# Fifteen loads of 1 to 15 short rows between the transfers of one DMA queue

## The chip, the cores and the metric

The kernel runs on one core of a Trainium2 chip. The metric is the device time of one execution in microseconds; the median of three runs is used.

## The reference

For each of 8 x 12 heads, Q, K and V are 512 x 64 in float32. The columns of Q and K are divided by their norms over the 512 rows, a 64 x 64 matrix is formed from them, a softmax runs over its last axis, and V is multiplied by the result:

```python
Q_norm = Q / (np.linalg.norm(Q, axis=-2, keepdims=True) + 1e-10)
K_norm = K / (np.linalg.norm(K, axis=-2, keepdims=True) + 1e-10)
attn = np.einsum('bhnd,bhne->bhde', Q_norm, K_norm)
attn = np.exp(attn - np.max(attn, axis=-1, keepdims=True))
attn = attn / (np.sum(attn, axis=-1, keepdims=True) + 1e-10)
return np.einsum('bhnd,bhde->bhne', V, attn)
```

Q, K and V are 12.58 MB each and so is the output: 50.3 MB pass between HBM and the core's SBUF, whatever the order of the work.

## The kernel before

The 96 heads are taken four at a time (24 units u), two units to a stage s (12 stages) and two stages to a pair w (6 pairs). A stage loads Q and K (`load_qk`, L172, one or two transfers for each), casts them to bfloat16 on VectorE (L212), forms the Gram matrices on TensorE (L232), takes norms and scores from them (L239 to L290), and multiplies by V, which `load_v` (L189) brings and which is cast (L168, L170) and transposed (L301) for it. ScalarE brings the products from PSUM (L166, L320) and `store` (L198) writes them out, 512 KB at a time.

All transfers but the first two loads of K are issued by SyncE, in one queue; those two go through ScalarE's queue. An object `Order` (L22) plans the order on every engine with costs written by hand, and the loop at L458 emits the pieces in that order. Four loads (`ahead`) are emitted before it, at L330. The loads from `HELD` on are kept back until the piece `UNTIL` has been emitted, and are then emitted in a row (L466).

The transfers are numbered here as the loop emits them: A1 to A4 are the four loads ahead of it, T1 to T67 the others, all from SyncE. T1 is the first load of V (1 MB), T2 to T5 are the four quarters of stage 1's Q and K (512 KB each), T6 is V (1 MB), T7 to T10 are the quarters of stage 2 (512 KB each), T11 to T22 are loads of 1 MB, T23 and T24 are the first two stores. A load of Q or K is 128 rows (a quarter) or 256 rows of 4 KB, a load of V 128 rows of 8 KB, a store 256 rows of 2 KB. One store near the end (T60 to T63, L202 to L204) is cut into 92, 4 and 32 rows and the other 128.

Completion is told by semaphores. The framework gives the transfers eight of them in turn, so that each transfer waits, at its issue on SyncE, until the transfer eight places ahead of it has landed, besides what its buffer needs. For the built program that reads, around the place of the change (lane numbers are the eight semaphores; the rows are the program's order on SyncE with their waits):

```
T5   L187 DMACopy qk<-in_K_dram 128x1024 [waits lane 0, DVE]
T6   L194 DMACopy v<-in_V_dram 128x2048 [waits lane 1]
T7   L187 DMACopy qk<-in_Q_dram 128x1024 [waits lane 2]
T8   L187 DMACopy qk<-in_K_dram 128x1024 [waits lane 3]
T9   L187 DMACopy qk<-in_Q_dram 128x1024 [waits lane 4]
T10  L187 DMACopy qk<-in_K_dram 128x1024 [waits lane 5]
T11  L185 DMACopy qk<-in_Q_dram 128x2x1024 [waits lane 6, DVE]
```

A transfer's rows are dealt out to as many as 16 DMA engines, each of which works through its share in order and then counts the semaphore up by one; the transfer has landed when the last engine has done so.

Of the kernel before, what the change touches and what calls it, by code (L numbers as in the profile page):

```python
# [8 lines left out]
F32 = mybir.dt.float32  # L9
# [4 lines left out]
D = 64  # L14
# [88 lines left out]
def kernel(  # L103
# [7 lines left out]
    nc = tc.nc  # L111
# [218 lines left out]
    for r in range(2):  # L330
# [7 lines left out]
        name=nc.get_next_instruction_name(), engine=mybir.EngineType.Activation, ins=[], outs=[], act_func_set_id=LN_EXP))  # L338
# [40 lines left out]
    def loaded(x, s, r):  # L379
        return ("l" + "qk"[x], s, r if len(parts(s)) == 2 else None)  # L380
# [33 lines left out]
    for w in range(W):  # L414
        both = 2 * w >= BOTH
        for r in range(2):
            halves = (None,)
            n = 2 * w + r - NB["v"]
# [22 lines left out]
    for s in range(S):  # L441
        for x in range(4):
            i, k = divmod(x, 2)
            n = 4 * s + x - 2
# [3 lines left out]
            n = 2 * s + i - NB["so"]  # L448
# [6 lines left out]

    ahead = [loaded(x, 0, r) for r in range(2) for x in range(2)]
    held, passed = [], False
    for (emit, eng), (_, _, key, _) in zip(plan.run(), plan.order):  # L458
        if eng == "DMA" and not passed and (held or key == HELD):
            held.append(emit)  # L460
            continue
        if key not in ahead:
            emit(eng)
        if key == UNTIL:
            passed = True
            for load in held:  # L466
                load("DMA")


# [28 lines left out]
```

## Time and profile before

| what | value |
|---|---|
| three runs, median (lowest to highest) | 129.33 us (129.22 to 129.61) |
| span of the profiled execution | 127.4 us |
| busy: VectorE, TensorE, ScalarE, GpSimd | 92.9, 77.0, 72.3, 37.0 us |
| moved | 50.66 MB, mean 398 GB/s |

The page gives no other time of the profiled execution than its span; the difference to the median of the runs, 1.9 us, lies around the span.

The trace also records each DMA packet and each step of a semaphore, which no view prints. Packets of the kernel's own queues have these durations (median):

| packet | count | ns |
|---|---|---|
| 4 bytes (semaphore step) | 1112 | 9 |
| 2,048 bytes (store row) | 6144 | 84 |
| 4,096 bytes (Q or K row) | 6144 | 159 |
| 8,192 bytes (V row) | 1536 | 309 |
| 16,384 bytes (a block of instructions, queue q8) | 17 | 935 |

And some transfers, in us from the start of the span: when SyncE began the issue, when the first of the 16 engines counted the semaphore up, and when the last did:

| transfer | issue begins | first engine done | last engine done |
|---|---|---|---|
| T3 | 2.85 | 12.62 | 13.05 |
| T4 | 3.33 | 13.87 | 15.45 |
| T5 | 6.70 | 15.13 | 16.69 |
| T6 | 7.08 | 17.58 | 19.13 |
| T7 | 8.46 | 18.83 | 20.35 |
| T8 | 8.83 | 20.06 | 21.57 |
| T9 | 10.61 | 21.32 | 23.16 |
| T10 | 11.82 | 22.58 | 24.23 |
| T11 | 13.12 | 25.05 | 26.68 |
| T13 | 16.70 | 30.02 | 31.70 |
| T17 | 23.22 | 39.89 | 41.48 |
| T18 | 25.66 | 42.38 | 44.02 |
| T21 | 32.38 | 49.86 | 51.40 |
| T22 | 34.21 | 52.34 | 53.88 |
| T28 | 51.05 | 64.79 | 66.58 |
| T29 | 51.77 | 67.28 | 70.22 |
| T30 | 53.90 | 69.78 | 72.67 |
| T57 | 106.62 | 113.83 | 116.85 |
| T58 | 107.89 | 115.12 | 119.65 |
| T59 | 109.22 | 116.39 | 120.69 |
| T67 (the last) | 120.75 | 123.55 | 126.53 |

For T67 the 16 engines ended at 123.6 (three), 124.3 to 125.5 (twelve) and 126.5 (one).

### The profile page before, as it was taken

To read this page: it belongs to the slowest core of one execution; us is meant where nothing else is said; L and a number is where in the kernel's file an instruction comes from. 1 tells how busy PE (TensorE), PEld (TensorE's weight loads), DVE (VectorE), ACT (ScalarE), POOL (GpSimd) and SP (SyncE) were. 2 spreads that over 40 slices of the span, in tenths; PEclk is the share of its full clock that TensorE was granted. 3 is DMA by queue.
4 is the path that set the end of the run, shared out by engine and by line. 5 is a ranking of instruction groups with operands and counts; after the bars stand their busy time and mean duration, and the time that the engine had idled before them with its cause. 6 is when DMAs were issued, how large, how long until landed. Compare 5 with 4: busy or idle time off the path is not lost.

```text
span 127.4 us, 4949 instructions
## 1 busy us (share of the span) xinstructions
PE 77.0 (60%) x2160; PEld 62.7 (49%) x2160; DVE 92.9 (73%) x142; ACT 72.3 (57%) x220; POOL 37.0 (29%) x39
## 2 busy tenths in 40 slices
PE   0065393994837679859475986777597729753000
PEld 0054372783636568647354674666386517541000
DVE  3344749949899899999974989998999499950000
ACT  4000441559877077886691897583848919996000
POOL 4006307300916903033077011303733160300000
PEclk9999999999985555999996799869959995999755
DMA  4999999999999999999999999999999999999991
GB/s 113 413 438 408 428 411 418 417 433 408 435 418 414 411 417 424 402 415 427 423 414 414 415 428 417 415 424 425 401 420 419 401 402 410 395 408 408 375 377 60
DMA packets 14958, 50.66 MB, mean 398 GB/s; under 512 B 1112, under 2 KB 1112, under 8 KB 13400
## 3 DMA queue, kind: packets, MB, share of 16 engines
q1 hardware_dynamic: 14648, 49.29, 95.9%
q10 hardware_dynamic: 288, 1.05, 2.1%
q8 instruction: 17, 0.28, 0.8%
q14 instruction: 5, 0.04, 0.1%
HBM read 37.75 MB, written 12.58 MB: 395 GB/s over the span
## 4 chain that ended last, share of the span: by engine, by line
DVE 36%; PE 21%; DMA 19%; issue 8%; ACT 5%; SPq 1%; DVEq 0%; ACTq 0%
DVE qkb L212 15%; DMA qk<-in_K_dram 14%; PE gram L232 12%; DVE scr L239 7%; DMA qk<-in_Q_dram 5%; DVE vt L168 4%; PE vps L301 4%; DVE ab L290 4%; PE po L318 3%; ACT so L166 3%; DVE n L251 2%; ACT ex L281 2%; DVE vb L168 2%; PE lg L275 1%; SPq L185 1%
## 5 line engine op out<-in xcount | busy, mean ns | idle before, releaser
L232 PE MATMUL gram<-qkb 32*128 32x128 bf16 x1536 | 36.7, 259 | 24.8 <-issue 8.5
L232 PEld LDWEIGHTS <-qkb 32*128 32x128 bf16 x1536 | 30.8, 116 | 29.7 <-issue 11.1
L212 DVE CAST qkb<-qk 128x1024 bf16<-128x1024 f32 x48 | 37.7, 810 | 9.6 <-DMA qk<-in_Q_dram 8.0
L170 POOL TENSOR_SCALAR vb<-v 128x1024 bf16<-128x1024 f32 x18 | 21.7, 1215 | 43.9 <-DMA v<-in_V_dram 39.0
L166 ACT COPY vt<-vps 128x1024 bf16<-128x1024 bf16 (+1 forms) x18 | 17.8, 986 | 18.8 <-PE vps L301 18.7
L166 ACT COPY so<-po 128x512 f32<-128x512 f32 x45 | 24.9, 593 | 6.1 <-PE po L318 5.8
L318 PE MATMUL po<-ab,vt 128*64 128x128 bf16 x384 | 19.1, 237 | 6.2 <-issue 2.6
L262 POOL TENSOR_TENSOR kqs<-kq,r 64x512 f32<-64x512 f32 x12 | 14.0, 1169 | 29.1 <-ACT r L258 16.2
L301 PE MATMUL vps<-identb,vb 128*128 128x128 bf16 x192 | 18.5, 253 | 4.8 <-POOL vb L170 3.5
L239 DVE SCALAR_TENSOR_TENSOR scr<-gram,eye 64x512 f32<-64x512 f32 x24 | 16.5, 687 | 4.9 <-PE gram L232 4.7
L318 PEld LDWEIGHTS <-vt 128*64 128x64 bf16 x384 | 13.4, 117 | 10.4 <-issue 5.7
L301 PEld LDWEIGHTS <-vb 128*128 128x128 bf16 x192 | 14.0, 113 | 7.9 <-POOL vb L170 4.2
L281 ACT ACTIVATE ex<-lg,rq 128x64 f32<-128x64 f32 x48 | 14.5, 322 | 2.7 <-PE lg L275 2.6
L166 ACT COPY kq<-gram 64x512 f32<-64x512 f32 x12 | 7.0, 582 | 13.2 <-DVE scr L239 12.9
L290 DVE TENSOR_TENSOR ab<-ex,rinv 64x256 bf16<-64x256 f32 x24 | 12.8, 534 | 0.6
L281 ACT ACTIVATION_READ_ACCUMULATOR ex<-lg,rq 128x1 f32 x48 | 10.2, 213 | 0.0
L168 DVE CAST vb<-v 128x1024 bf16<-128x1024 f32 x6 | 7.4, 1241 | 1.8 <-DMA v<-in_V_dram 1.7
L275 PE MATMUL lg<-eye,kqs 64*128 64x64 f32 x48 | 6.4, 259 | 3.2 <-issue 1.6
L251 DVE TENSOR_REDUCE n<-scr 128x8 f32<-128x512 f32 x12 | 8.1, 679 | 0.1
L168 DVE COPY vt<-vps 128x1024 bf16<-128x1024 bf16 (+1 forms) x8 | 8.0, 1022 | 0.2
L275 PEld LDWEIGHTS lg<-eye,kqs 64*128 64x128 f32 x48 | 4.5, 156 | 5.0 <-issue 2.5
L287 DVE RECIPROCAL rinv<-esum 128x4 f32<-128x4 f32 x12 | 2.0, 170 | 2.5 <-ACT ex L281 2.4
(17 smaller groups left out, 16.0 us busy)
## 6 DMA issues: line engine op xcount, KB each, us to landing
v<-in_V_dram SPq DMA_DIRECT2D x12, 1024.0 KB, 17.4
out_dram<-so SPq DMA_DIRECT2D x23, 512.0 KB, 11.2
qk<-in_Q_dram SPq DMA_DIRECT2D x8, 1024.0 KB, 16.8
qk<-in_K_dram SPq DMA_DIRECT2D x8, 1024.0 KB, 18.8
qk<-in_Q_dram SPq DMA_DIRECT2D x8, 512.0 KB, 11.9
qk<-in_K_dram SPq DMA_DIRECT2D x6, 512.0 KB, 12.6
qk<-in_K_dram ACTq DMA_DIRECT2D x2, 512.0 KB, 7.3
out_dram<-so SPq DMA_DIRECT2D x1, 256.0 KB, 7.2
```

The costliest lines, as they stand in the source:

```text
L166: nc.scalar.copy(o, i)
L168: nc.vector.tensor_copy(o, i)
L170: nc.gpsimd.tensor_scalar(out=o, in0=i, scalar1=1.0, scalar2=0.0, op0=ALU.mult, op1=ALU.add)
L212: nc.vector.tensor_copy(qkb[u][:, :, x * D:(x + 1) * D], qk32[s][:, x, r])
L232: nc.tensor.matmul(gram[s][:, h, r, 0], x, x, start=(t == 0), stop=(t == (T if u < WIDE else J) - 1))
L239: nc.vector.scalar_tensor_tensor(out=scr[s][half], in0=gram[s][half, :, :, 0, half].rearrange("p h r d -> p (h r) d"), scalar=1e-20, in1=e ...
L262: (nc.vector if eng == "DVE" else nc.gpsimd).tensor_tensor(out=kqs[s][HI], in0=kq[s][HI], in1=r8[s][HI, :, None].to_broadcast([D, 2 * HU, ...
L275: nc.tensor.transpose(l[:, h, :], kqs[s][HI, 2 * h:2 * h + 2].rearrange("p r d -> p (r d)"), eye2[HI])
L281: nc.scalar.activation(e[:, h, :], lg[s][:, h, :], AF.Exp, scale=rq[s][:, h:h + 1], accum_out=z[:, h:h + 1])
L290: nc.vector.tensor_tensor(out=a[half, :, half], in0=e[half], in1=ri[half, :, None].to_broadcast([D, HU, D]), op=ALU.mult,)
L301: nc.tensor.transpose(ps[:, c, n, :], vb[w][:, J * c + j].rearrange("p r d -> p (r d)"), identb)
L318: nc.tensor.matmul(po[s, x][e * D:(e + 1) * D, j].rearrange("p r d -> p (r d)"), v, ab[s][:, h, :])
```

## The change

Behind each of the seventh to the 21st transfer that the loop emits (T7 to T21) one small load is issued on SyncE: the n-th takes the first 16 floats (64 bytes) of the first n rows of K into the first n partitions of a tile of its own, which nothing reads. These loads take their turn among the eight semaphores like the others. They make 120 rows, 7,680 bytes, and the tiles take 15 x 64 bytes of each partition of SBUF.

```diff
     held, passed = [], False
+    marks = ctx.enter_context(tc.tile_pool(name="marks", bufs=1))
+    Km = K.rearrange("b h n d -> (b h n) d")
+    seen = [0]
+
+    def mark():
+        seen[0] += 1
+        n = seen[0] - 6
+        if 0 < n < 16:
+            m = marks.tile([128, D // 4], F32, name=f"mark{n}")
+            nc.sync.dma_start(out=m[0:n], in_=Km[0:n, 0:D // 4])
+
+    def emit_dma(emit):
+        emit("DMA")
+        mark()
+
     for (emit, eng), (_, _, key, _) in zip(plan.run(), plan.order):
...
         if key not in ahead:
-            emit(eng)
+            emit_dma(emit) if eng == "DMA" else emit(eng)
         if key == UNTIL:
             passed = True
             for load in held:
-                load("DMA")
+                emit_dma(load)
```

In the built program the order on the other engines is the same as before, and on SyncE the fifteen loads M1 to M15 stand where the diff says. Around the first of them, with the semaphore each waits for:

```
T7   L187 DMACopy qk<-in_Q_dram 128x1024 [waits lane 2]
M1   L467 DMACopy mark<-in_K_dram 1x16 [waits lane 3]
T8   L187 DMACopy qk<-in_K_dram 128x1024 [waits lane 4]
M2   L467 DMACopy mark<-in_K_dram 2x16 [waits lane 5]
T9   L187 DMACopy qk<-in_Q_dram 128x1024 [waits lane 6]
M3   L467 DMACopy mark<-in_K_dram 3x16 [waits lane 7]
T10  L187 DMACopy qk<-in_K_dram 128x1024 [waits lane 0]
M4   L467 DMACopy mark<-in_K_dram 4x16 [waits lane 1]
T11  L185 DMACopy qk<-in_Q_dram 128x2x1024 [waits lane 2, DVE]
```

## Prediction

> **What bounds the kernel now.** First the page: its span, the slices, and the queues.
>
> ```profile
> span 127.4 us, 4949 instructions
> ...
> DMA  4999999999999999999999999999999999999991
> ...
> q1 hardware_dynamic: 14648, 49.29, 95.9%
> ...
> DVE 36%; PE 21%; DMA 19%; issue 8%; ACT 5%; SPq 1%; DVEq 0%; ACTq 0%
> ```
>
> The DMA engines are busy in all slices but the first and the last, and the kernel's own queue q1 alone takes 95.9% of the 16 engines' span. The chain of waits in the fourth of these lines gives VectorE 36%, but it ends with a copy at 116.6 us, before the last stores drain, so it isn't what ends the kernel. The windows by stage settle it (the columns are the stretch, its length, busy us of PE, PEld, DVE, ACT and POOL with counts, granted clock, DMA share, GB/s):
>
> ```profile
> 12.00:24.00 12.00, 6.81 (x188) 5.64 (x192) 9.29 (x16) 4.67 (x18) 4.09 (x4) 1.00 1.02 418
> 24.00:36.00 12.00, 9.42 (x298) 7.58 (x291) 9.42 (x13) 8.48 (x24) 4.30 (x4) 1.00 1.03 424
> ...
> 120.00:124.00 4.00, 0.00 (x0) 0.00 (x0) 0.00 (x0) 0.00 (x0) 0.00 (x0) 0.50 0.98 380
> ```
>
> The DMA share is 1.0 in each stretch from 2 us on, while no other engine is full in the stretches of the change; from 120 us on nothing else works. So the end is set by the transfers' sum on the DMA engine that ends last: 126.53 us for T67, with the next one at 125.5. Two things can move it: work added to that engine, or a time in which it has nothing queued.
>
> For the second the issues matter. SyncE's own timeline (start, us taken, line, what):
>
> ```profile
> 8.83 0.43 SPq L187 DMA_DIRECT2D qk<-in_K_dram  x1
> 10.61 0.33 SPq L187 DMA_DIRECT2D qk<-in_Q_dram  x1
> 11.82 0.33 SPq L187 DMA_DIRECT2D qk<-in_K_dram  x1
> 13.12 0.38 SPq L185 DMA_DIRECT2D qk<-in_Q_dram  x1
> ...
> 53.90 0.38 SPq L185 DMA_DIRECT2D qk<-in_K_dram  x1
> ```
>
> These are T8 to T11 and T30. T9 starts at 10.61, where T1, eight places ahead, landed at 10.59; T10 at 11.82 (T2: 11.80); T30 at 53.90 (T22: 53.88). Eight transfers are in flight and the ninth waits for the first of them. T9 then lands at 23.16, 12.6 us after its issue, though its own 8 rows an engine take 8 x 159 ns = 1.27 us: over 11 us of it is queue. That queue is the cover that the change eats into.
>
> **The change part by part.** Nothing is removed, and the transfers keep their order.
>
> *Work on the DMA engines.* A row of 2,048, 4,096 and 8,192 bytes takes 84, 159 and 309 ns: 9 ns and 0.0366 ns a byte. No row has 64 bytes; the nearest are the semaphore step below (4 bytes, 9 ns) and the store row above (84 ns), and the line through them gives 9 + 64 x 0.0366 = 11 ns. I take that, since these sizes lie on one line. With its semaphore step a small row costs an engine 20 ns (18 to 93 by the two ends). 120 of them are 120 x 20 = 2.4 us, over 16 engines 0.15 us each. If M-n lies on n engines from one end, that end gets 15 x 20 = 0.30 us, the other none. Which engine ends last I can't name from a view, but it isn't among those that took the 92-row store: their semaphore steps for that store (four, at 118.3 to 119.5) continue from 116.4 to 117.6 at T59, while the late one did T58 at 119.65. It thus gets 0 to 11 small rows; I take four, 4 x 20 = 0.08 us, ends 0 and 11 x 93 = 1.0 us. The engines of the 92-row store, at most 125.5 at the end, have 1.0 us to spare and get at most 0.30 by the price taken.
>
> By the Trainium skill (DMA: Bandwidth & Descriptors, "Why a DMA increments its semaphore by 16 and not by 1") a transfer runs on the largest number up to 16 that divides its rows, on the lowest-numbered engines. The trace agrees as to the number: the 92-row store posted four single steps, as 92 = 4 x 23. By it engine 0 gets all fifteen small rows and engine 15 none, the 0.30 us above; a spread over all engines would give 0.15 us to the last one too, and 0.15 for my 0.08 in the sum.
>
> *SyncE.* Each small load takes an issue, 0.33 to 0.43 us by the rows above, 15 x 0.4 = 6 us between 8.8 and 44 us, in which SyncE mostly waits. They also take fifteen of the places among eight. So T8 to T22 wait for the transfer four or so before, not eight, in the sense that half of the eight in flight are small. Go through it with the table's landings: M1 waits for A4 and T8 for T1 (10.59, was issued at 8.83); T9 for T3 (13.05, was 10.61); T10 for T5 (16.69, was 11.82); T11 for T7 (20.35, was 13.12); T12 for T8 (21.57); T17 for T13 (31.70, was 23.22); T22 for T18 (44.02, was 34.21). After that the eight places fill again: T30 waits for T22 (53.88) as before and begins at 53.9 as before, and nothing differs from there on.
>
> *Does an engine run dry?* T11 is the tightest. The fastest engine is through with T10 at 22.58, the slowest at 24.23. From issue to first packet takes 1.03 us (first issue 0.74, first packet of q1 1.77), so T11 can flow from 20.35 + 1.03 = 21.38: 1.2 us before the fastest and 2.85 us before the slowest engine needs it. T17: the first engine needs it at 37.4 (T16, one transfer of 2.5 us before 39.89); it is there at 32.7, 4.7 us early. T22: needed at 49.86, there at 45.05, 4.8 us early. So all lateness is absorbed, and loads land when they did; VectorE, TensorE and the stores don't notice. If the cover were gone, each us that the last engine stands dry is a us at the end. Value taken: 0, as 0 lies nearer to these covers; the other end is T11's whole delay, 20.35 - 13.12 = 7.2 us, which the 11 us of queue exclude.
>
> Sum: 127.4 + 0.08 = 127.5 us of span; with the 1.9 us between span and median, 129.4 us.
>
> **The rivals.**
>
> *The queue runs dry (slower).* Place: T11, behind four half-size transfers with four small ones between, where least is queued. For it: lag to landing falls from 13.2 us (13.5 to 26.7) to about 6. Against: the 1.2 and 2.85 us above. It decides from a response (landing to first packet of the transfer that waited) of 1.03 + 2.85 = 3.9 us on, or sooner for the fast engines, which have 1.0 us to spare at the end: 1.03 + 1.2 + 1.0 = 3.2 us. At a response of 4 us the fast ones lose 1.8, 0.8 more than they can spare: 130.2 us.
>
> *Small rows are dear.* If a 64-byte row costs an engine what a store row does, 93 ns with its step, seven of them (half of the possible 0 to 11, and one more) are 0.65 us: 130.0 us. For: no row that short is in the trace. Against: the straight line, whose fixed part is 9 ns. The Trainium skill (the same page, "Specifications") says that under 512 bytes an engine reads, changes and writes back; no run here shows that yet, and my estimate of what it would make is this rival's time.
>
> *Blocks of instructions fall elsewhere.* A block of 16 KB sets one engine back by some 1.4 us: one packet at 13.15, and the spread of a landing goes from 0.43 (T3) to 1.58 (T4). The seventeen go round few engines: at 66.1 one is hit twice (spread 1.79 at T28, 2.94 at T29), and that at 117.65 takes T58 from 3.0 to 4.5. That last one makes the late engine. Were it to fall on an engine with one block less, the next in line would end the kernel, 125.5: 1.0 us less, 128.4. Were the fifteen further instructions of SyncE to bring a block of 8 KB onto the late engine, 0.3 us more, 129.7. For: SyncE's program is longer. Against: the blocks are TensorE's almost wholly (4,320 of 4,949 instructions), whose order stays.
>
> *The change doesn't do what it says* can't well be: the built program has the loads in their places.
>
> **How the numbers follow.** Forecast 0.64; dry queue 0.08; dear rows 0.12; blocks 0.16, of which 0.07 to the faster side. A measurement of this kernel can tell about 0.3% from no change, 0.39 us. The forecast's own range is 129.1 to 129.7, nearly all of it no change: same 0.60, slower 0.03, faster 0.01. Adding the rivals: slower 0.03 + 0.08 + 0.12 + 0.09 = 0.32; faster 0.01 + 0.07 = 0.08. The range reaches from 129.0 (the runs' own 0.1 below the median, and some of the faster side) to 130.2 (the dear rows and the dry queue).
>
> **What would show it.** On the changed kernel's page: q1 with 14648 + 240 packets and 1112 + 240 under 512 bytes; DMA at 9 in the same 38 slices; T11 issued near 20.4 instead of 13.12 while its cast starts as before; the median to landing of 1 MB loads some us shorter; and the issues equal again from 53.9 on. A slice of the first half with DMA below 9 would show a dry queue. A last engine later by more than 0.3 us at unchanged order, with the lag growing through 20 to 55 us, would show dear rows; a lag that appears in one step, a block. I am wrong if the median is off by over 0.4 us.

## The result and the profile after

| | before | changed |
|---|---|---|
| median of 18 runs each | 129.31 us | 130.06 us |
| lowest to highest | 128.91 to 129.63 | 129.27 to 130.76 |
| ratio, 95% interval | | 1.0056, 1.0037 to 1.0075 |
| profiled execution: time, span | span 127.4 us | 129.42 us, span 127.6 us |

The change costs 0.56%, some 0.7 us, where 0.1 was forecast, and the runs now spread over 1.5 us instead of 0.7. The profiled execution, at 129.42 us, is one of the fastest of the changed kernel; most of the 0.7 us isn't in it, and two more profiles of the same kernel stand below. Of the five runs with two more loads (below), two, at 132.55 and 132.82 us, lie over 1.5% above the fastest; they are left out of its ratio, and its profile, which is of the first of them, isn't used.

The page of the changed kernel (span; busy tenths of the DMA engines and GB/s in 40 slices; packets; queue q1; two rows of the issues, with the median from issue to landing at the end):

```profile
span 127.6 us, 4964 instructions
...
DMA  3999999999999999999999999999999999999992
GB/s 105 407 435 409 424 416 414 379 421 409 432 418 415 410 413 423 407 413 424 426 421 406 419 416 425 411 429 419 401 419 418 406 401 408 401 406 398 402 369 111
DMA packets 15198, 50.66 MB, mean 397 GB/s; under 512 B 1352, under 2 KB 1352, under 8 KB 13640
...
q1 hardware_dynamic: 14888, 49.30, 96.1%
...
v<-in_V_dram SPq DMA_DIRECT2D x12, 1024.0 KB, 10.5
...
qk<-in_K_dram SPq DMA_DIRECT2D x8, 1024.0 KB, 10.6
```

The packets are those forecast, 240 more in q1 and under 512 bytes. A V load now lands 10.5 us after its issue, before 17.4: the queue in front of it is that much shorter. The DMA row is full, but the GB/s row isn't: the eighth slice, 22.3 to 25.5 us, has 379 where the page of before has 417. The busy row counts a packet as long as it is open, and some were open long: of the 374 packets of 4,096 bytes begun from 22 to 26 us 16 took over 300 ns, before 2 of 410, with a median of 159 ns in both. So the busy row doesn't show this loss; the bytes do. SyncE's timeline of the changed kernel at that place (start, us, line, what):

```profile
16.72 0.33 SPq L187 DMA_DIRECT2D qk<-in_K_dram  x1
19.17 0.27 SPq L467 DMA_DIRECT2D mark<-in_K_dram  x1
20.44 0.38 SPq L185 DMA_DIRECT2D qk<-in_Q_dram  x1
20.87 0.38 SPq L467 DMA_DIRECT2D mark<-in_K_dram  x1
21.62 0.81 SPq L185 DMA_DIRECT2D qk<-in_K_dram  x1
```

These are T10, M4, T11, M5 and T12 (L467 is the line of the small loads). T11 goes out at 20.44, 7.3 us later than before, right behind the landing of T7 (20.38). The same windows in both kernels, first before, then the changed one (stretch, length, busy us of PE, PEld, DVE, ACT, POOL with counts, granted clock, DMA share, GB/s):

```profile
22.00:24.00 2.00, 1.68 (x53) 1.42 (x55) 1.95 (x4) 1.41 (x4) 0.00 (x0) 1.00 1.03 416
24.00:26.00 2.00, 1.98 (x52) 1.52 (x47) 1.37 (x1) 0.61 (x3) 1.04 (x1) 1.00 1.03 424
```

```profile
22.00:24.00 2.00, 1.00 (x28) 0.73 (x30) 1.97 (x5) 1.61 (x3) 0.00 (x0) 1.00 1.01 375
24.00:26.00 2.00, 2.00 (x60) 1.80 (x48) 1.15 (x2) 0.78 (x4) 1.43 (x1) 1.00 1.03 391
```

(416 - 375 + 424 - 391) x 2 us is 148 KB not moved in these 4 us, 0.35 us at 420 GB/s. That is where the time begins to go.

### The profile page after: what moved, and what is told of

Same layout as the page of the kernel before. It is cut to its first block, busy times and chain, and to the rows that moved or that the text cites. A ratio compares the mean times of both kernels' runs of the same rounds, so it can differ in the third digit from the quotient of the medians.

```text
span 127.6 us, 4964 instructions
## 1 busy us (share of the span) xinstructions
PE 80.3 (63%) x2160; PEld 65.6 (51%) x2160; DVE 91.7 (72%) x142; ACT 72.6 (57%) x220; POOL 37.0 (29%) x39
## 3 DMA queue, kind: packets, MB, share of 16 engines
q10 hardware_dynamic: 288, 1.05, 2.1%
## 4 chain that ended last, share of the span: by engine, by line
DMA 50%; DVE 17%; PE 13%; issue 5%; ACT 5%; SPq 1%; DVEq 0%; ACTq 0%
DMA qk<-in_K_dram 36%; DMA qk<-in_Q_dram 14%; PE gram L232 5%; DVE vt L168 4%; PE po L318 4%; DVE qkb L212 4%; PE vps L301 3%; DVE ab L290 2%; ACT so L166 2%; DVE vb L168 2%; DVE scr L239 2%; SPq L185 1%; DVE n L251 1%; PE lg L275 1%; ACT ex L281 1%
## 5 line engine op out<-in xcount | busy, mean ns | idle before, releaser
L212 DVE CAST qkb<-qk 128x1024 bf16<-128x1024 f32 x48 | 35.4, 761 | 10.1 <-DMA qk<-in_Q_dram 7.2
L318 PE MATMUL po<-ab,vt 128*64 128x128 bf16 x384 | 21.9, 263 | 5.8 <-DVE ab L290 1.8
L318 PEld LDWEIGHTS <-vt 128*64 128x64 bf16 x384 | 15.9, 134 | 10.4 <-issue 5.5
L290 DVE TENSOR_TENSOR ab<-ex,rinv 64x256 bf16<-64x256 f32 x24 | 14.2, 592 | 0.6
L275 PE MATMUL lg<-eye,kqs 64*128 64x64 f32 x48 | 6.9, 273 | 4.5 <-POOL kqs L262 3.1
L168 DVE CAST vb<-v 128x1024 bf16<-128x1024 f32 x6 | 6.9, 1150 | 2.3 <-DMA v<-in_V_dram 2.2
## 6 DMA issues: line engine op xcount, KB each, us to landing
v<-in_V_dram SPq DMA_DIRECT2D x12, 1024.0 KB, 10.5
```

The source lines that it names most:

```text
L168: nc.vector.tensor_copy(o, i)
L212: nc.vector.tensor_copy(qkb[u][:, :, x * D:(x + 1) * D], qk32[s][:, x, r])
L275: nc.tensor.transpose(l[:, h, :], kqs[s][HI, 2 * h:2 * h + 2].rearrange("p r d -> p (r d)"), eye2[HI])
L290: nc.vector.tensor_tensor(out=a[half, :, half], in0=e[half], in1=ri[half, :, None].to_broadcast([D, HU, D]), op=ALU.mult,)
L318: nc.tensor.matmul(po[s, x][e * D:(e + 1) * D, j].rearrange("p r d -> p (r d)"), v, ab[s][:, h, :])
```

## The experiments

Two theories: the queue runs short at T11 (it is issued late, as it waits for T7, because M1 to M4 hold four of the eight places), or the small loads cost by themselves, by their rows on the DMA engines or by their number. All times are medians, with the ratio to the runs of before that were made beside them.

**Four loads alone.** The loads behind T11 to T21 are left out.

```diff
-        if 0 < n < 16:
+        if 0 < n < 5:
```

> Only M1 to M4 are issued (10 rows, behind T7 to T10); M5 to M15 are left out. T11 still has to wait for T7. If the loss is the queue running short at T11 (in the changed kernel's profile 375 and 391 GB/s in 22 to 26 us against 416 and 424 before): the whole loss stays, about 130.0 us (+0.7, ratio 1.005). If it is the DMA engines' work on small rows: 10 of 120 rows stay, below 0.1 us, 129.4. If it is the count of small loads on SyncE or in the semaphores: 4 of 15, +0.2, 129.5.

129.76 us (129.24 to 130.79), ratio 1.0038 (1.0016 to 1.0059). Four loads with 10 of 120 rows make two thirds of the loss; the whole of it, which was expected, also lies within the interval. Their profile has the gap (two of its windows):

```profile
22.00:24.00 2.00, 1.68 (x50) 1.42 (x52) 2.00 (x4) 1.33 (x3) 0.00 (x0) 1.00 0.98 377
24.00:26.00 2.00, 1.99 (x52) 1.53 (x48) 1.37 (x2) 0.57 (x3) 1.04 (x1) 1.00 1.04 416
```

**The other eleven alone.** M1 to M4 are left out.

```diff
-        if 0 < n < 16:
+        if 4 < n < 16:
```

> Only M5 to M15 (110 rows, behind T11 to T21). T11 waits as before the change. If the loss is the queue running short at T11: no more than the rows' own time stays, 129.3 to 129.5, and 22 to 26 us are at 416 to 424 GB/s again. If it is the work on small rows: 110 of 120 rows, nearly all of the loss, 130.0 us. If the count: 11 of 15, +0.5, 129.8.

129.51 us (129.26 to 129.84), ratio 1.0011 (1.0000 to 1.0022). 110 of 120 rows make a fifth of the loss, and the two windows are back at 414 and 420 GB/s.

**One row each.**

```diff
-            nc.sync.dma_start(out=m[0:n], in_=Km[0:n, 0:D // 4])
+            nc.sync.dma_start(out=m[0:1], in_=Km[0:1, 0:D // 4])
```

> All fifteen loads, each of one row instead of 1 to 15, so 15 rows instead of 120. Queue short at T11: unchanged, 130.0. Work on small rows: with one row each on one engine, about as much on that engine but 15 of 120 in all, so 129.4 unless that engine is the last one. Count of loads: unchanged, 130.0.

130.13 us (129.87 to 131.06), ratio 1.0067 (1.0041 to 1.0092). With an eighth of the rows the loss is no smaller. The rows are not it; their number of loads could still be.

**All fifteen, later.** Behind T24 to T38.

```diff
-        n = seen[0] - 6
+        n = seen[0] - 23
```

> All fifteen loads with their 1 to 15 rows, but behind T24 to T38 instead of T7 to T21, where transfers of 1 MB stand in the queue. Queue short at T11: that is gone, so only the rows' own time stays, 129.3 to 129.6. Work on small rows or count of loads: the same loss as in the changed kernel, 130.0.

129.47 us (129.16 to 129.76), ratio 1.0008 (0.9997 to 1.0020). The number isn't it either: the place is.

**Three loads.** M1 to M3, one load fewer than in the first experiment.

```diff
-        if 0 < n < 16:
+        if 0 < n < 4:
```

> Only M1 to M3 (6 rows, behind T7 to T9): one load fewer than the run with M1 to M4. By the places, T11 now waits for T6 (19.2 us) and not for T7 (20.4 to 20.6), while T8 to T10 are as late as there. Queue short at T11: with a response of about 2.2 us its packets start at 21.4, before the first engine is done with T10 (22.3), so nothing is lost: 129.3 to 129.5. If each small load costs its share: three quarters of the run with four, 129.65.

129.44 us (129.34 to 129.63), ratio 1.0007 (0.9998 to 1.0016). The fourth load makes the whole step. SyncE's timeline with three loads (M3, T10, T11, T12), and the window:

```profile
15.79 0.26 SPq L467 DMA_DIRECT2D mark<-in_K_dram  x1
17.00 0.33 SPq L187 DMA_DIRECT2D qk<-in_K_dram  x1
19.51 0.38 SPq L185 DMA_DIRECT2D qk<-in_Q_dram  x1
20.68 0.37 SPq L185 DMA_DIRECT2D qk<-in_K_dram  x1
```

```profile
22.00:24.00 2.00, 1.68 (x46) 1.41 (x49) 2.00 (x4) 1.22 (x3) 0.00 (x0) 1.00 1.03 412
```

T11 waits for T6 and goes out at 19.51, 0.9 us earlier than in the changed kernel's profile; that suffices, and 412 GB/s are kept.

**More behind T10.** M1 to M4, and two or four more loads of four rows behind T10 (the diff is that with two; with four more, 5 stands for 3).

```diff
-        if 0 < n < 16:
-            m = marks.tile([128, D // 4], F32, name=f"mark{n}")
-            nc.sync.dma_start(out=m[0:n], in_=Km[0:n, 0:D // 4])
+        if 0 < n < 5:
+            for c in range(3 if n == 4 else 1):
+                m = marks.tile([128, D // 4], F32, name=f"mark{n}_{c}")
+                nc.sync.dma_start(out=m[0:n], in_=Km[0:n, 0:D // 4])
```

> M1 to M4, and two more loads of four rows behind T10, so that T11 waits for T8 (21.7 us) in place of T7. Queue short at T11: its packets start near 23.8, the fast engines stand 1.4 us, the one late engine (done with T10 at 24.1) not at all; the fast ones end about 1 us before the late one otherwise, so the end moves by 0.5 to 1.2 us: 129.9 to 130.6, and T11's landings draw together. If the loss is per load or per row: 6 loads, 18 rows, 129.6.

> M1 to M4, and four more loads of four rows behind T10, so that T11 waits for T9 (23.2 us). Queue short at T11: its packets start near 25.3, the fast engines stand 3 us and the late one 1.2 us; the end moves by 1.5 to 2.3 us: 130.9 to 131.7. Per load or per row: 129.7.

Two more: three runs of 130.57 to 130.97 us, ratio 1.0109 (1.0089 to 1.0128), 1.4 us, a little over what was expected. Four more: 131.61 us (131.48 to 132.12), ratio 1.0174 (1.0157 to 1.0191), 2.2 us. The loss grows with T11's lateness, not with the loads: 8 loads cost three times what all fifteen do. With four more, SyncE issues M4 and its four companions, then T11 at 23.38, and the engines stand:

```profile
19.25 3.04 SPq L468 DMA_DIRECT2D mark<-in_K_dram  x5
23.38 0.40 SPq L185 DMA_DIRECT2D qk<-in_Q_dram  x1
```

```profile
20.00:22.00 2.00, 0.66 (x5) 0.40 (x6) 1.96 (x3) 0.58 (x1) 1.68 (x2) 1.00 1.04 420
22.00:24.00 2.00, 1.68 (x50) 1.41 (x51) 2.00 (x4) 1.34 (x4) 0.00 (x0) 1.00 0.30 109
24.00:26.00 2.00, 1.98 (x52) 1.52 (x44) 1.33 (x2) 0.60 (x3) 1.04 (x1) 1.00 0.70 188
```

From 420 GB/s to 109 and 188: a gap at the same place as in the changed kernel, wide open. Here the engines do stand empty, and the DMA share (0.30, 0.70) shows it.

**Four behind T10.** None behind T7 to T9, so T8 to T10 go out nearly as early as before (9.03, 10.80 and 12.01 for 8.83, 10.61 and 11.82).

```diff
-        if 0 < n < 16:
-            m = marks.tile([128, D // 4], F32, name=f"mark{n}")
-            nc.sync.dma_start(out=m[0:n], in_=Km[0:n, 0:D // 4])
+        if n == 4:
+            for c in range(1, 5):
+                m = marks.tile([128, D // 4], F32, name=f"mark{c}")
+                nc.sync.dma_start(out=m[0:c], in_=Km[0:c, 0:D // 4])
```

> M1 to M4 all behind T10, none behind T7 to T9: T8 to T10 are issued as early as before the change, T11 waits for T7 as in the run with M1 to M4 between. Queue short at T11 alone: the same loss as that run, 129.8 to 130.0. If the lateness of T8 to T10 makes the loss: 129.4.

130.13 us (129.32 to 131.00), ratio 1.0045 (1.0022 to 1.0069), the loss of the run with four between, within the intervals. The lateness of T8 to T10 adds nothing that shows, and the window has the gap again:

```profile
22.00:24.00 2.00, 0.93 (x25) 0.67 (x27) 1.97 (x4) 1.59 (x2) 0.00 (x0) 0.50 0.95 326
```

**All fifteen, one transfer later.** Behind T8 to T22.

```diff
-        n = seen[0] - 6
+        n = seen[0] - 7
```

> All fifteen loads with their 120 rows, each one transfer later (behind T8 to T22 in place of T7 to T21). T11 then waits for T6 (19.2 us) and not for T7 (20.4 to 20.9). Queue short at T11: no loss but the rows' own time, 129.35 to 129.6, and narrow runs. If count, rows or the lateness of the other transfers count too: like the changed kernel, 130.0.

129.53 us (129.30 to 129.67), ratio 1.0015 (1.0005 to 1.0024). The same loads and rows, moved by one place, lose a quarter of what they lost: 0.2 us in place of 0.7. T11, the third line here, again goes out behind T6, and here a small load (M3) stands right in front of it:

```profile
15.46 0.33 SPq L187 DMA_DIRECT2D qk<-in_K_dram  x1
16.68 0.26 SPq L467 DMA_DIRECT2D mark<-in_K_dram  x1
19.18 0.38 SPq L185 DMA_DIRECT2D qk<-in_Q_dram  x1
```

```profile
22.00:24.00 2.00, 1.68 (x59) 1.44 (x60) 1.80 (x3) 1.64 (x5) 0.21 (x1) 0.50 1.02 402
24.00:26.00 2.00, 1.99 (x52) 1.53 (x44) 1.09 (x1) 0.61 (x2) 0.83 (x1) 0.50 1.03 418
```

**128 rows each, later.** The price of a row, at the place where the loads cost nearly nothing else.

```diff
-        n = seen[0] - 6
+        n = seen[0] - 23
...
-            nc.sync.dma_start(out=m[0:n], in_=Km[0:n, 0:D // 4])
+            nc.sync.dma_start(out=m[0:128], in_=Km[0:128, 0:D // 4])
```

> Fifteen loads of 128 rows of 64 bytes, 8 for each engine, behind T24 to T38, where fifteen loads of 1 to 15 rows cost 0.1 us. A row at 11 ns and a step at 9 ns: 15 x (8 x 11 + 9) = 1.5 us on each engine, 130.8 to 131.0. Rows at the price of a store row, 84 ns: 15 x (8 x 84 + 9) = 10.2 us, 139.6.

130.43 us (130.22 to 130.76), ratio 1.0091 (1.0072 to 1.0111), less than the 130.8 to 131.0 that the packets' 11 ns had given. 1.1 us for 120 rows and 15 semaphore steps on each engine; with the steps at 9 ns a row costs (1130 - 135) / 120 = 8 ns. Its 1,920 packets of 64 bytes show 11 ns each; the difference isn't explained.

**The changed kernel again, twice,** unedited, for more profiles.

> The changed kernel once more, for a second profiled execution: the first one was at 129.42 us one of its fastest (median 130.06). In the profiles of three variants that were slow (M1 to M4, one row each, four behind T10) the mean landing over the 16 engines lost 0.3 to 0.4 us at T11 and T12 and another 0.3 at T22, which stood in the queue for over 8 us; the first profile of the changed kernel has the former alone. If that is what parts its executions: at 130.0 us or more, T22 comes 2.7 us or more after T21 in the mean, and at 129.5 or less 2.5. If the loss at T11 alone varies: 130.0 us goes with 0.7 us or more at T11, and T22 stays at 2.5.

> The changed kernel a third time, with the same two expectations: an execution of 130.0 us or more shows the further 0.3 us at T22, one of 129.5 or less doesn't; or else the loss at T11 alone grows with the time.

Their executions took 129.83 and 129.65 us. Both lie between the times of which the expectations speak (130.0 and 129.5), so neither is decided by them. The mean landing over the 16 engines, from the trace's semaphore steps, in us; the cover is the time from T11's issue to the first engine's step for T10:

| profile | T11 issued | cover | T10 to T11 | T11 to T12 | T21 to T22 | T10 to T67 |
|---|---|---|---|---|---|---|
| before | 13.12 | 9.46 | 2.49 | 2.49 | 2.47 | 102.0 |
| eleven (M5 to M15) | 13.17 | 9.56 | 2.48 | 2.51 | 2.46 | 102.1 |
| one later | 19.18 | 3.35 | 2.54 | 2.53 | 2.46 | 102.2 |
| three | 19.51 | 3.02 | 2.51 | 2.50 | 2.44 | 102.0 |
| changed, 129.42 us | 20.44 | 2.06 | 2.74 | 2.64 | 2.47 | 102.4 |
| changed, 129.65 us | 20.40 | 2.15 | 2.96 | 2.63 | 2.56 | 102.6 |
| changed, 129.83 us | 20.52 | 1.84 | 2.93 | 3.16 | 2.46 | 103.1 |
| four | 20.61 | 2.00 | 2.72 | 2.54 | 2.80 | 102.6 |
| four behind T10 | 20.61 | 1.97 | 2.91 | 2.52 | 2.74 | 102.7 |
| one row each | 20.85 | 1.69 | 2.86 | 2.60 | 2.76 | 102.8 |
| four and four more | 23.38 | -0.83 | 5.07 | 2.61 | 3.03 | 105.2 |

Where the cover is 3.0 us or more, nothing is lost; at 2.2 and below, T11 comes 0.2 to 0.5 us late in the mean (2.6 with four and four more). To this every such profile adds a second loss, 0.1 to 0.7 us at T12 or 0.3 to 0.6 at T22, at a place that changes. No run delays T11 without small loads; but neither their rows, nor their number, nor one right in front of T11 makes the loss where T11 is in time. Both together make the 0.4 to 1.1 us by which the changed kernel's last column exceeds 102.0. So T22 doesn't part the changed kernel's executions; the sum of the losses does, in these three.

## Why the prediction was right in its range and wrong in its working

The measured 130.06 us lies within 129.0 to 130.2, but the upper end of that range came from two rivals. The forecast's own 129.4 missed by 0.66 us, more than the 0.4 that it named as the sign of being wrong, and its own range of 129.1 to 129.7 missed too. That the wider range held is luck: the loss was put at 0 for a reason that failed.

- **What bounds the kernel** held: the loss appears where the DMA engines move fewer bytes, and in the table the loss at T11 and behind it is never made good.
- **The places.** Right, to 0.2 us at first: T8, T9, T10, T11 and T12 were to be issued at 10.59, 13.05, 16.69, 20.35 and 21.57, and were at 10.74, 13.20, 16.72, 20.44 and 21.62. T22 came at 44.75 (44.02 foretold) and T30 at 54.68, not at 53.90 as before, each behind the landing that it waits for, which was by then 0.7 to 0.8 us late.
- **The rows.** Right in size: 64-byte packets take 11 ns as the line through the longer ones gave, and where only rows and steps cost, the fifteen loads cost 0.1 to 0.2 us (ratios 1.0008 and 1.0015). The rival of dear rows is out: 128 rows each would have given 139.6 at 84 ns a row, and gave 130.43. The Trainium skill (DMA: Bandwidth & Descriptors, "Specifications") has line rate from 512 bytes on; the trace agrees so far, as 64 bytes in 11 ns are 5.8 GB/s an engine against 26.5 for a V row, but a price beyond that doesn't show.
- **Does an engine run dry? This step failed.** It took 1.03 us from issue to first packet, measured at the start, for the time in which a transfer takes effect, and so found T11 1.2 us early for the fastest engine and put the loss at 0. Two things were wrong in that sum. The engine runs out before its semaphore step shows it: T67's last packet in the profile before ended at 126.19, its step came at 126.53, 0.33 us later. And the first packet isn't the flow: with four more loads, where all engines had emptied, T11's first packet came 1.05 us after its issue (24.43), but twelve of the packets begun from 24.66 to 24.90 took 425 to 1,052 ns for 159. T11's first engine's step came 4.30 us after its issue (27.68), of which 2.47 us are its 16 rows; that leaves 1.83 us. So against 1.83 us the covers of 1.7 to 2.15 us in the table are no margin, where 1.03 had left 1.2 (T10's first step 22.58 - 21.38). A loss of 0.2 to 0.5 us at a cover of 2 us is more than even 1.83 us gives. The packets show where it goes: in the changed kernel's first profile the engines hardly stand (DMA share 1.01 and 1.03, before 1.03 and 1.03), but the time beyond 159 ns of the packets begun from 22 to 26 us sums to 0.34 us an engine (before 0.03), most of the 0.40 us lost at T11 and T12. Why packets are slow when T11 goes out this late stays open.
- **The 2.85 us of the slowest engine, and the 1.0 us that the fast ones have to spare.** Half right: from T10's last step to T11's last there is no loss (24.31 to 26.76 in the first profile of the changed kernel, 2.45 us, as before). But this didn't protect the end. T67's last step came at 126.6 in that profile, 126.8 and 127.1 in the two others, and 127.2 to 127.4 in the three variants with T11 late by its wait for T7, against 126.5 to 126.8 where T11 was in time. Why the last engine loses too was not settled; the engines can't be told apart by name in the records.
- **The rival** that named the place and the late issue, the dry queue at T11, came nearest, at 130.06 us for 130.2, though in the changed kernel the engines had slow packets rather than none. It was given a chance of 0.08, because it was to decide only from a response of 3.2 us on; in the runs the loss set in between a cover of 3.0 us and one of 2.2. The rival of instruction blocks wasn't needed: both pages have 17 of them. The sign named for the dry queue, a slice with the DMA row below 9, was the wrong one: the row stayed at 9, and the GB/s told it.

## What to carry to other kernels

A small transfer in a queue with a fixed number of places costs its place more than its bytes: count what is in flight in us of work, at the place with the shortest transfers, and keep some 3 us of it beyond the issue of the next one (the least that cost nothing here). The same loads beside transfers of twice the size, or one place further on, cost about a quarter or less. A busy share of 1.0 doesn't prove that the queue was full; compare the bytes moved slice by slice.

## What the runs showed of the hardware

The second loss was unexpected. In four of the profiles with T11 late, a transfer that had long been queued came slowly: T22 took 2.74 to 2.80 us in the mean in three of them (3.03 with four and four more), with 8 to 12 of its 8,192-byte packets at over 500 ns for 309, though it had been issued 5 us or more before they began; in the changed kernel's execution of 129.83 us two 4,096-byte packets begun at 24.83 and 24.98, where T12 follows T11, took 1.8 and 1.9 us for 159 ns. In the profiles with T11 in time T22 took 2.44 to 2.47 us. The Trainium skill (DMA: Bandwidth & Descriptors, "Latency and other measured facts") gives 2 us for an access to HBM under high load, which is the size of these two packets; what makes them slow, no run here tests. Engines brought into step by the gap don't fit: the fourteen that end T11 first lie within 0.44 us before (25.05 to 25.49), and within 1.23 us in the changed kernel's first profile (25.29 to 26.52). Slow packets may also widen the runs, which no run here tests: those of variants with T11 in time lie within 0.3 to 0.6 us, those with T11 late by the wait for T7 within 1.2 to 1.7.
